# Row scales issued inside the projection, the second decay and the key packing earlier, forget gates and transposed copies on ScalarE

## The chip, the cores and the metric

The kernel runs on one core of one Trainium2 chip. The metric is device time in microseconds of one execution. A core has five engines that matter here: TensorE (PE, matmuls; its weight loads are listed as PEld), VectorE (DVE), ScalarE (ACT), GpSimd (POOL) and SyncE (SP, which issues nearly all DMAs). Each works through its own queue in order; an instruction whose operands aren't there holds up everything behind it in its queue.

## The reference

Two layers over 256 tokens of width 2048, in FP32: layer 0 mixes with HGRN2, layer 1 with gated linear attention (GLA); each also attends to 256 memory tokens, and is followed by a SwiGLU FFN.

```python
def _chunk_gated_linear_attention(q, k, v, log_a):   # S_t = diag(a_t) S_{t-1} + k_t v_t^T ; o_t = S_t^T q_t
...
def _hgrn2_mixer(hn, w_in, lb, onorm):
    proj = hn @ w_in
    q, f, i, g, xq = jnp.split(proj, [...], axis=-1)
    f = lb + (1.0 - lb) * jax.nn.sigmoid(f.astype(f32))
    log_f = jnp.log(f)
    k = 1.0 - f
    q = jax.nn.silu(q.astype(f32))
    o = _chunk_gated_linear_attention(q, k, i, log_f)            # 12 heads of 128
    y = _gated_head_norm(o, onorm, g, HGRN_HEADS)

def _gla_mixer(hn, w_in, w_gk, b_gk, onorm):
    proj = hn @ w_in
    q, k, v, g, gk_low, xq = jnp.split(proj, [...], axis=-1)
    log_a = jax.nn.log_sigmoid((gk_low @ w_gk + b_gk).astype(f32)) / 16
    o = _chunk_gated_linear_attention(q * DK ** -0.5, k, v, log_a)  # 4 heads
    y = _gated_head_norm(o, onorm, g, GLA_HEADS)
...
for layer in range(DEPTH):
    hn = _rmsnorm(h, norm_mix[layer])
    y, xq = mixer(hn)
    xa = _memory_attention(xq, mem_n, w_mem_kv[layer])           # softmax(q k^T) v over the memory
    h = h + jnp.concatenate([y, xa], axis=-1) @ w_out[layer]
    hn = _rmsnorm(h, norm_ffn[layer])
    gate, up = jnp.split(hn @ w_gate_up[layer], 2, axis=-1)
    h = h + (jax.nn.silu(gate) * up) @ w_down[layer]
return _rmsnorm(h, norm_final)
```

## The kernel before

**Products.** Every FP32 product is made from rounded parts: a weight chunk `raw` that a DMA brought is cast by ACT (`CAST parts<-raw`, the high half) and DVE subtracts (`parts<-raw,parts`, the low half); PE then does three products (high by high, high by low, low by high), the high half first. The parts lie in a ring of six buffers, the raw chunks in one of three. Some weight columns are worked in a form with fewer products (names with c and d, such as parts34c and parts34d), for which DVE adds and subtracts raw chunks first (`raw<-raw`).

**Order.** In the FFN the order of the instructions is kept as written. In the mixers a list scheduler orders each engine's queue by the program's dependences and its own estimates, so that an edit in one place can change the order elsewhere. Side work is queued with `later(...)` and issued piece by piece between the weight chunks of a projection.

**Row scales.** The RMS norm's row factor r is not applied to h but to the outputs of a projection. `h_scale` sums the squares (`rx_red`, `rm_red` on DVE), turns them with two tiny matmuls on PE (`rx_back`, `rm_back`) and makes r (`rx_v`, `rx_r`; `rm_v`, `rm_r`). rx belongs to layer 0, whose first projection is `hx`; rm to layer 1, whose first is `gx`, behind the last FFN product `fd`.

**HGRN.** Three groups of four heads. The group's gates `fs` and queries `qs` get their activations on ACT (each with an ACT_TABLE_LOAD), are turned by PE (`tf`, `tq`), and become `F` (the forget gate), `K` = 1 - F and `Q`. `decays` multiplies F into a tree (`Th`). `gated_scores` then makes the scores by levels: the even diagonal (`slh` with `k1h`), pairs (`sph`), levels 2 to 6 (`slh`), and `across` (`pxh`); `place` copies each into `sch` by mask, `grow` multiplies K and Q by the next product of decays, and `pack` copies the keys of the next level into a home, which is half of F, from the third level on. Values `vs` and `gates` come from the same projection (`hv0p` to `hv2p`; `hf1p` and `hf2p` are the next group's).

**GLA.** Two pairs of heads with the same scores (`GF`, `GK`, `GQ`, `Tg`, `slg`, `scg`). `decay(pr)` makes GF out of the matmuls `zp`: abs (`ab`) and min, Exp, Ln, a subtraction, Exp. decay(0) is issued behind the attention, decay(1) behind the scores of pair 0. The readout `gpo` gets its squares from ACT (`junk_go`), its factor (`gro_v`, `gro_r`), the gate (`ggate`), and PE turns it (`ty`).

**Attention to the memory.** Turned keys `kT`, queries `xT` and probabilities `pT` come out of PSUM by DVE copies, two of 128x512 each.

The lines named L151 in the profile are a wrapper that issues every instruction; the tile names tell them apart.

Of the kernel before, what the change touches and what calls it, by code (L numbers as in the profile page):

```python
# [17 lines left out]
P = 128  # L18
# [22 lines left out]
def trunk_kernel(ctx: ExitStack, tc: tile.TileContext, x, mem, norm_mix, norm_ffn, norm_mem,  # L41
# [694 lines left out]
    for l in range(2):  # L736
        kv = side([P, 2, XH * T], f"kv{l}")
        kT.append(kv[:, 0, :].rearrange("p (h t) -> p h t", t=T))
        vm.append(kv[:, 1, :].rearrange("p (m c) -> p m c", c=XA))
        ks = work.tile([P, NT, XA], F32, tag="stg", name=f"ks{l}", bufs=2)  # L740
        project_two(memq["pairs"], MEM[l], w_mem_kv[l], 0, XA, XA, f"m{l}",
                    lambda: [lambda t: ks[:, t, :], lambda t: vm[l][:, t, :]], prep=prep_mem if l == 0 else None)
        if l == 0:
            later(*[lambda p=p: more_of(memq, p, "hq", f"mem{p}") for p in range(len(PAIRS))
                    if f"{p}S" in MEM[1] and f"{p}S" not in MEM[0]])
            rm = mem_scale()
            load_params()
            hq, ss, first_turns = {}, new_ss("ss_x"), []
            for q in range(NQ):

                h_quad(hq, q, g_mix[0], ss, "hx", later if q > 1 else first_turns.append)
        for d in (ks, vm[l]):
            for t in range(NT):
                ac.activation(out=d[:, t, :], in_=d[:, t, :], func=AF.Copy, scale=rm[:, t:t + 1])

        def turn_keys(l=l, ks=ks):
            for j in range(2):
                tp = transposes([lambda t, c=2 * j + i: ks[:, t, c * P:(c + 1) * P] for i in range(2)], f"tk{l}{j}")
                ve.tensor_copy(kT[l][:, 2 * j:2 * j + 2, :].rearrange("p h t -> p (h t)"), tp)

        later(turn_keys)

# [4 lines left out]
    def attention(l, ps, r, yq):  # L767
# [7 lines left out]
        def turn_queries():  # L775
            st["xT"] = xT = work.tile([P, XH, T], F32, tag="Q", name=f"xT{l}")
            for j in range(2):
                tp = transposes([lambda t, c=2 * j + i: xs[:, t, c * P:(c + 1) * P] for i in range(2)], f"tx{l}{j}", True)
                ve.tensor_copy(xT[:, 2 * j:2 * j + 2, :].rearrange("p h t -> p (h t)"), tp)

        def softmax(t):
            xT = st["xT"]
# [20 lines left out]
        def turn_probs(m):  # L803
            pT = st["pT", m] = work.tile([P, XH, T], F32, tag=("T", "sc")[m], name=f"pT{l}{m}")
            for j in range(2):
                tp = transposes([lambda t, c=2 * j + i: st["prob", t][:, c, m * P:(m + 1) * P] for i in range(2)],
                                f"ap{l}{m}{j}")
                ve.tensor_copy(pT[:, 2 * j:2 * j + 2, :].rearrange("p h t -> p (h t)"), tp)

        def mix():  # L810
            quad = yq[3] = Quad("tq", f"y{l}_3")
# [13 lines left out]
    def decays(st, F, name):  # L825

        n = F.shape[2]
        st["F"] = F
        tots = work.tile([P, n * T], F32, tag="T", name=f"T{name}")
        st["T"] = {1: F.rearrange("p t n c -> p (t n c)")}  # L830
        at = 0
        for m in LEVELS[:-1]:
            tv = st["T"][m].rearrange("p (b o) -> p b o", o=2)
            nb = n * T // (2 * m)
            st["T"][2 * m] = tots[:, at:at + nb]
            ve.tensor_tensor(out=st["T"][2 * m], in0=tv[:, :, 0], in1=tv[:, :, 1], op=ALU.mult)
            at += nb

    def put_queries(st, Q, n0, ps, scale):

        n, ns = 2, Q.shape[3]
        q0, q1 = n0 * P, (ns * NT + n0) * P
        tq, tp, c = ns * P, n * P, (2, n * P // 2)
        ac.activation(out=at(Q, q0, (tq + 1, NT), c), in_=at(ps, 0, (tp + 1, NT), c), func=AF.Copy, scale=scale)
        ac.activation(out=at(Q, q1 + 2, (tq - 2, NT), (4, n * P // 4), (1, 2)),
                      in_=at(ps, 1, (tp - 1, NT), (4, n * P // 4), (2, 2)), func=AF.Copy, scale=scale)
        ve.scalar_tensor_tensor(out=at(Q, q0 + 1, (tq - 1, NT), c), in0=at(ps, 1, (tp - 1, NT), c), scalar=scale,
                                in1=at(st["T"][2], n0 * P // 2, (tq // 2, NT), (1, n * P // 2)), op0=ALU.mult, op1=ALU.mult)  # L850

    def gated_scores(st, heads, name):

# [26 lines left out]
            mult(K, 0, n * P + m, 1, n * P // m)  # L880
            mult(Q, q, n * P + m - q, 0, n * P // m + 1)

        def pack(m, home):

            n = st["K"].shape[2]
            nb = n * P // (2 * m)
            ac.copy(out=at(home, 0, (m, NT), (2 * m, nb), (1, m)), in_=at(st["K"], 0, (n * P + m, NT), (2 * m, nb), (1, m)))
            st["keys"] = home

        def score(ps, keys, q, i, parts):  # L890
            pe.matmul(ps, keys, q, start=i == 0, stop=i == len(parts) - 1)

# [8 lines left out]
        def even_diagonal():  # L901
            sc = st["sc"] = work.tile([P, ng, P], F32, tag="sc", name=f"sc{name}")
            nc.gpsimd.memset(sc, 0.0)
            pack(1, work.tile([P, st["K"].shape[2], P], F32, tag="scx", name=f"k1{name}"))
            ps = both(1, 0, 1)
            for t in range(NT):
                place(t, 0, ps[:, :, t, :], 1)
            grow(1)

        def pairs():  # L910
            for t in range(NT):
                ps = aux_ps(f"sp{name}{t}").rearrange("p (g x c) -> p g x c", x=2, c=64)
                for a, parts in enumerate(heads):
                    for i, f in enumerate(parts):
                        q = st["Q"][:, :, t, f, :].rearrange("p x (b o m) -> p x b o m", o=2, m=2)[:, :, :, 1 - t, :]
                        score(ps[:, a, :, :].rearrange("p x (b m) -> p x b m", m=2), st["K"][:, t, f, :], q, i, parts)
                place(t, 1, ps[:, 0:nh, 1, :], 1)
                place(t, 2, ps[:, 0:nh, 0, :], 2)
            grow(2)
            pack(4, st["F"][:, 1])  # L920

        def level(li):
            m = LEVELS[li]
            ps = both(m, m, -m)
            grow(m)
            if li + 1 < len(LEVELS):
                pack(2 * m, st["F"][:, li % 2])
            for t in range(NT):
                place(t, 1 + li, ps[:, :, t, :], m)

# [21 lines left out]
    def hgrn_group(w, g, hq, r, yq):  # L952
# [19 lines left out]
        def turn_f():  # L972
            F = work.tile([P, NT, 4, P], F32, tag="F", name=f"F{g}")
            K = st["K"] = work.tile([P, NT, 4, P], F32, tag="K", name=f"K{g}")
            for j in range(2):
                tp = transposes([lambda t, c=2 * j + i: fs[:, t, c * P:(c + 1) * P] for i in range(2)], f"tf{g}{j}")
                for i in range(2):
                    c = 2 * j + i
                    ve.tensor_scalar(out=F[:, :, c, :], in0=tp[:, i * T:(i + 1) * T].rearrange("p (t c) -> p t c", c=P),
                                            scalar1=oml[:, 4 * g + c:4 * g + c + 1],  # L980
                                            scalar2=lb[:, 4 * g + c:4 * g + c + 1], op0=ALU.mult, op1=ALU.add)
            ve.tensor_scalar(out=K, in0=F, scalar1=-1.0, scalar2=1.0, op0=ALU.mult, op1=ALU.add)
            decays(st, F, f"h{g}")

        def turn_q():
# [24 lines left out]
        v, gate = stages("----SSS-" if g < 2 else "----SS--", (2 * MIX, "v", AF.Copy), (3 * MIX, "gate", AF.Silu))  # L1010
        later(*([None, None, read, None, turn_y] if g < 2 else [read, None, turn_y]))

    def hgrn(hq, r, yq):
        w = hgrn_w_in[0]
        later(*first_turns)
        ps = project(hq, (2, 3, 0, 1), w, 4 * MIX, XA, "hx")
        attention(0, [[(0, ps[t])] for t in range(NT)], r, yq)
        for g in range(3):
            hgrn_group(w, g, hq, r, yq)
# [1 line left out]
    def gla_pair(w, pr, dec, decay, hq, r, yq):  # L1021
# [4 lines left out]
        def turn_k():  # L1026
            decays(st, dec[pr], f"g{pr}")
            K = st["K"] = work.tile([P, NT, 4, P], F32, tag="K", name=f"GK{pr}")
            for j in range(2):
                tp = by_tiles([lambda t, i=i: ks[:, t, j, i * P:(i + 1) * P] for i in range(2)], f"tgk{pr}{j}")  # L1030
                ac.copy(out=K[:, :, 2 * j:2 * j + 2, :].rearrange("p t h c -> p t (h c)"), in_=tp.rearrange("p (t c) -> p t c", t=NT))

        def turn_q():
            Q = st["Q"] = work.tile([P, 2, NT, 4, P], F32, tag="Q", name=f"GQ{pr}")
# [38 lines left out]
        ks, qs = dst  # L1073
        scores = gated_scores(st, [[0, 1], [2, 3]], f"g{pr}")
        if pr == 0:
            scores += [None, lambda: decay(1)]
        later(None, None, turn_k, turn_q, None, *scores)
        GLA = (("-----SS-", "-----SS-"), ("-----SS-", "-----SS-"))
        gate, v = [], []
# [10 lines left out]
                    ac.activation(out=dst[:, t, :], in_=dst[:, t, :], func=func, scale=r[:, t:t + 1])  # L1090
            later(None, None, lambda a=a: read(a), None, lambda a=a: turn_y(a))

    def gla(hq, r, yq):
        w = gla_w_in[0]
        half = (GR + XA) // 2
        kv = side([P, 2, XH * T], "kv")
# [4 lines left out]
        wgk = gk[:, 0:4, :]  # L1101
        nc.gpsimd.memset(wgk, 0.0)
        nc.sync.dma_start(out=wgk[0:GR, :, 0:DK], in_=gla_w_gk[0].rearrange("r (h c) -> r h c", c=DK))
        psx = [project(hq, range(NQ), w, 3 * MIX + i * half, half, f"gx{i}") for i in range(2)]
        low = gk[:, 4, :].rearrange("p (t c) -> p t c", c=P)
        nc.gpsimd.memset(low, 0.0)
        for t in range(NT):
# [145 lines left out]


    flush()
    r = h_scale(ss, "rx", True)
    for l in range(2):
        yq = {}
        (hgrn if l == 0 else gla)(hq, r, yq)
        hq2, ss2 = {}, new_ss(f"ss_f{l}")  # L1260
        quad_pairs(yq)
        mores = [lambda p=p, tag=tag: more_of(yq, p, tag, f"y{l}_{p}", turned[0])
# [28 lines left out]
        if l == 0:  # L1291
            hq = {}
            ffn(0, hq2, r2, lambda n: h_quad(hq, n, g_mix[1], ss, "hm1_", sevens=2))
            r = h_scale(ss, "rm1", True)
        else:
            gf = []

# [76 lines left out]
```

## Time and profile before

| | |
|---|---|
| median of 3 runs | 2276.36 us (2274.17, 2276.36, 2276.65) |
| profiled execution | 2274.12 us, span 2272.3 us, granted clock 0.999 |
| PE busy | 2250.2 us, 99% of the span |
| DVE busy | 2087.6 us, 92% |
| ACT busy | 1423.8 us, 63% |
| POOL busy | 35.3 us, 2% |
| HBM | 430.71 MB read, 191 GB/s over the span |

A row of the timeline reads: start, duration (both in us), engine, line, operation, output<-inputs, tile and shape, how many were run together, and in brackets the idle time of the engine just before it with what ended that. Layer 0's mixer lies at about 100 to 470 us of the span, layer 1's at 1215 to 1500, the FFNs behind each.

### The profile page before, as it was taken

The page shows a single profiled execution, that of the slowest core. Times are in us where ns is not written, and L with a number is a line of the kernel's source. Part 1 is how long each engine was busy: PE and PEld are TensorE (multiplying, and loading weights), DVE is VectorE, ACT ScalarE, POOL GpSimd, SP SyncE. Part 2 cuts the span into 40 slices and gives each one's busy share as a digit, 9 for nine tenths or more (in the row PEclk, how much of TensorE's full clock was granted, in tenths as well). Part 3 has the DMA queues.
Part 4 walks back from the last instruction along what each step waited for, and adds up shares of the span by engine and source line. Part 5 has one row for each costly group of instructions (what it writes and reads, how often), then busy time and mean ns, then how long its engine had stood idle before and what let it go on. Part 6 is the DMA issues. An engine that isn't in the chain of part 4 may idle for free.

```text
span 2272.3 us, 29336 instructions
## 1 busy us (share of the span) xinstructions
PE 2250.2 (99%) x10710; PEld 1900.9 (84%) x10710; DVE 2087.6 (92%) x2635; ACT 1423.8 (63%) x1940; POOL 35.3 (2%) x41
## 2 busy tenths in 40 slices
PE   9999999999999999999999999999999999999998
PEld 7888888888888888888888999988888888888887
DVE  7889999899999999999996887889899999999997
ACT  6656656566666666666665666566566666666664
POOL 0000000000000000000000000001000000000000
PEclk9999999999999999999999999999999999999999
DMA  7645545555556665556655446455555565665664
GB/s 289 204 154 179 190 161 168 179 173 186 186 195 213 207 214 191 204 192 213 207 204 161 145 140 195 152 178 204 194 196 202 205 210 196 204 206 201 205 211 158
DMA packets 232645, 435.78 MB, mean 192 GB/s; under 512 B 13200, under 2 KB 42676, under 8 KB 232244
## 3 DMA queue, kind: packets, MB, share of 16 engines
q1 hardware_dynamic: 231203, 429.64, 56.1%
q10 hardware_dynamic: 1296, 4.26, 0.5%
q8 instruction: 84, 1.38, 0.2%
q14 instruction: 62, 0.50, 0.1%
HBM read 430.71 MB, written 3.15 MB: 191 GB/s over the span
## 4 chain that ended last, share of the span: by engine, by line
PE 90%; DVE 6%; ACT 2%; issue 1%; DMA 1%; POOL 0%; SPq 0%; POOLq 0%; DVEq 0%; ACTq 0%
PE f_p L151 38%; PE fd L151 19%; PE wo L151 4%; PE m1p L151 2%; PE hf0p L151 2%; PE wo0p L151 2%; PE wo1p L151 2%; PE fd_0p L151 2%; PE gk1p L151 1%; PE gg11p L151 1%; PE gg10p L151 1%; PE m0p L151 1%; DVE raw L151 1%; PE gg00p L151 1%; PE gx L151 1%
## 5 line engine op out<-in xcount | busy, mean ns | idle before, releaser
L151 DVE TENSOR_TENSOR raw<-raw 128x512 f32<-128x512 f32 (+3 forms) x474 | 402.8, 850 | 9.4 <-DMA raw<-in_hgrn_w_in_dram 0.2
L151 DVE TENSOR_TENSOR parts<-raw,parts 128x1024 fp32r<-128x1024 f32 (+1 forms) x216 | 246.1, 1179 | 17.0 <-ACT parts L151 16.8
L151 ACT CAST parts<-raw 128x1024 fp32r<-128x1024 f32 (+1 forms) x216 | 211.6, 1016 | 46.0 <-PE gx L151 8.1
L151 ACT COPY h<-fd 128x512 f32<-128x512 f32 x80 | 46.1, 590 | 52.3 <-PE fd L151 49.5
L151 ACT ACTIVATE s<-s,rf_r 128x512 f32<-128x512 f32 x44 | 31.8, 722 | 43.7 <-DVE s L151 43.7
L151 DVE TENSOR_TENSOR e<-f_p,e 128x512 f32<-128x512 f32 x66 | 45.1, 684 | 2.3
L151 ACT COPY fd<-h 128x512 f32<-128x512 f32 x82 | 45.2, 583 | 0.0
L151 PE MATMUL fd<-parts,s_0h 128*128 128x512 f32 x128 | 39.8, 392 | 0.0
L151 PE MATMUL fd<-parts,s_6h 128*128 128x512 f32 x128 | 39.8, 392 | 0.0
L151 PE MATMUL fd<-parts,s_2h 128*128 128x512 f32 x128 | 39.8, 392 | 0.0
L151 PE MATMUL fd<-parts,s_4h 128*128 128x512 f32 x128 | 39.8, 392 | 0.0
L151 PE MATMUL fd<-parts,s_8h 128*128 128x512 f32 x128 | 39.8, 392 | 0.0
L151 PE MATMUL fd<-parts,s_5h 128*128 128x512 f32 x128 | 39.4, 389 | 0.0
L151 PE MATMUL fd<-parts,s_7h 128*128 128x512 f32 x128 | 39.4, 389 | 0.0
L151 PE MATMUL fd<-parts,s_1h 128*128 128x512 f32 x128 | 39.4, 389 | 0.0
L151 PE MATMUL fd<-parts,s_3h 128*128 128x512 f32 x128 | 39.4, 389 | 0.0
L151 DVE TENSOR_TENSOR s<-f_p,e 128x512 f32<-128x512 f32 x44 | 30.3, 688 | 4.3 <-PE f_p L151 2.4
L151 DVE SCALAR_TENSOR_TENSOR s<-e,rf_r,s 128x512 f32<-128x512 f32 x44 | 31.0, 744 | 0.2
L151 PEld LDWEIGHTS fd<-parts,s_7h 128*128 128x128 f32 x128 | 24.0, 188 | 5.0
L151 PEld LDWEIGHTS fd<-parts,s_5h 128*128 128x128 f32 x128 | 24.0, 188 | 5.0
L151 PEld LDWEIGHTS fd<-parts,s_1h 128*128 128x128 f32 x128 | 24.0, 188 | 5.0
L151 PEld LDWEIGHTS fd<-parts,s_3h 128*128 128x128 f32 x128 | 24.0, 188 | 5.0
(5722 smaller groups left out, 7229.6 us busy)
## 6 DMA issues: line engine op xcount, KB each, us to landing
raw<-in_w_gate_up_dram SPq DMA_DIRECT2D x352, 512.0 KB, 3.9
raw<-in_w_down_dram SPq DMA_DIRECT2D x80, 1024.0 KB, 5.5
raw<-in_hgrn_w_in_dram SPq DMA_DIRECT2D x96, 512.0 KB, 3.9
raw<-in_gla_w_in_dram SPq DMA_DIRECT2D x96, 384.0 KB, 3.4
raw<-in_w_out_dram SPq DMA_DIRECT2D x16, 1024.0 KB, 6.0
raw<-in_w_out_dram SPq DMA_DIRECT2D x32, 512.0 KB, 4.1
raw<-in_w_mem_kv_dram SPq DMA_DIRECT2D x30, 512.0 KB, 5.5
raw<-in_w_down_dram SPq DMA_DIRECT2D x16, 512.0 KB, 4.5
```

Of the source, the lines that this page charges most:

```text
L151: ins = func(*args, **kwargs)
```

## The change

Row scales: the two calls of `h_scale` ahead of the layers go; the mixer calls it through `prep` inside its first projection. Second decay: decay(1) goes from the end of pair 0's scores to between levels 2 and 3. Key packing: `first_keys` packs k1 where K is made; the later homes are halves of Q that are no longer read, not of F. ACT instead of DVE: F and K of HGRN, and the copies of kT, xT and pT.

```diff
-                ve.tensor_copy(kT[l][:, 2 * j:2 * j + 2, :].rearrange("p h t -> p (h t)"), tp)
+                ac.copy(out=kT[l][:, 2 * j:2 * j + 2, :].rearrange("p h t -> p (h t)"), in_=tp)
...
+    def first_keys(st, name):
+        pack(st, 1, work.tile([P, st["K"].shape[2], P], F32, tag="scx", name=f"k1{name}"))
...
-            pack(4, st["F"][:, 1])
+            pack(st, 4, st["Q"][:, 1, 1])
...
-                pack(2 * m, st["F"][:, li % 2])
+                pack(st, 2 * m, st["Q"][:, 1, li % 2])
...
-                    ve.tensor_scalar(out=F[:, :, c, :], in0=tp[:, i * T:(i + 1) * T].rearrange("p (t c) -> p t c", c=P),
-                                            scalar1=oml[:, 4 * g + c:4 * g + c + 1],
-                                            scalar2=lb[:, 4 * g + c:4 * g + c + 1], op0=ALU.mult, op1=ALU.add)
-            ve.tensor_scalar(out=K, in0=F, scalar1=-1.0, scalar2=1.0, op0=ALU.mult, op1=ALU.add)
+                    ac.activation(out=F[:, :, c, :], in_=tp[:, i * T:(i + 1) * T].rearrange("p (t c) -> p t c", c=P), func=AF.Identity,
+                                  scale=oml[:, 4 * g + c:4 * g + c + 1], bias=lb[:, 4 * g + c:4 * g + c + 1])
+            ac.activation(out=K.rearrange("p t n c -> p (t n c)"), in_=F.rearrange("p t n c -> p (t n c)"), func=AF.Identity,
+                          scale=-1.0, bias=1.0)
+            first_keys(st, f"h{g}")
             decays(st, F, f"h{g}")
...
-        ps = project(hq, (2, 3, 0, 1), w, 4 * MIX, XA, "hx")
+        got = []
+        ps = project(hq, (2, 3, 0, 1), w, 4 * MIX, XA, "hx", prep=lambda q: q == 1 and got.append(scale()))
+        r, = got
...
-            scores += [None, lambda: decay(1)]
+            scores[5:5] = [lambda: decay(1), None]
...
-        psx = [project(hq, range(NQ), w, 3 * MIX + i * half, half, f"gx{i}") for i in range(2)]
+        got = []
+        psx = [project(hq, range(NQ), w, 3 * MIX + i * half, half, f"gx{i}",
+                       prep=lambda q: len(got) == 0 and q == 3 and got.append(scale())) for i in range(2)]
+        r, = got
...
-    r = h_scale(ss, "rx", True)
+    scale = lambda ss=ss: h_scale(ss, "rx", True)
...
-            r = h_scale(ss, "rm1", True)
+            scale = lambda ss=ss: h_scale(ss, "rm1", True)
```

What this does to the queues is seen at three places. The first is PE at the seam of the layers: `fd` is the last product of layer 0's FFN, `gx` the first of layer 1. Before:

```order
L151 MATMUL fd_5_3_0_1_9664<-parts_2_9722,s_10h 128x512 x2
L151 MATMUL fd_5_3_0_1_9664<-parts_2_9722,s_10l 128x512
L151 MATMUL rm_back<-rm_red,ident 128x2
L151 MATMUL rm_back<-rm_red,turned_id 128x2
L151 MATMUL gx_0_0_9769<-parts_0_9773,hm_0x 128x264 x3
L151 MATMUL gx_0_1_9770<-parts_0_9773,hm_0x 128x264 x3
```

Now rm_back stands inside gx, behind its products with hm_5:

```order
L151 MATMUL gx_0_0_9760<-parts_2_9851,hm_5x 128x264 x3
L151 MATMUL gx_0_1_9761<-parts_2_9851,hm_5x 128x264 x3
L151 MATMUL rm_back<-rm_red,ident 128x2
L151 MATMUL rm_back<-rm_red,turned_id 128x2
L151 MATMUL gx_0_0_9760<-parts_0_9889,hm_6x 128x264 x3
```

The two matmuls moved behind the products of gx with hm_0 to hm_5.

The second place is the head of the first HGRN group on ACT. Before:

```order
L151 ACTIVATE qs_1519<-qs_1519,rx_r 128x512 x2
L151 CAST parts30b<-raw_1681 128x1024
L151 ACTIVATE Q_1612<-tq_1613 128x2x128
L151 ACTIVATE Q_1612<-tq_1613 128x2x64x2
L151 COPY k1h_1658<-K_1583 128x2x256
L151 CAST parts31a<-raw_1731 128x1024
```

Now:

```order
L151 ACTIVATE qs_1519<-qs_1519,rx_r 128x512 x2
L151 ACTIVATE F_1582<-tf_1584,lbt 128x2x128 x2
L151 ACTIVATE F_1582<-tf_1591,lbt 128x2x128 x2
L151 ACTIVATE Q_1614<-tq_1615 128x2x128
L151 ACTIVATE K_1583<-F_1582 128x1024
L151 ACTIVATE Q_1614<-tq_1615 128x2x64x2
L151 COPY k1h_1599<-K_1583 128x2x256
L151 CAST parts30b<-raw_1681 128x1024
```

F and K came in behind the activation of the queries, and the cast of parts30b moved behind them and behind k1h. In the second group the same stands on ACT, and DVE's order changes too where its values and gates are put together. Before:

```order
L151 TENSOR_TENSOR gates_2706<-hv1p_2611,vs_2705 128x512
L151 TENSOR_TENSOR parts52a<-raw_2754,parts52a 128x1024
L151 TENSOR_TENSOR vs_2705<-hv1p_2607,gates_2706 128x512
L151 TENSOR_TENSOR Q_2413<-Q_2413,Th_2400 128x2x32x8
L151 TENSOR_TENSOR gates_2706<-hv1p_2603,vs_2705 128x512
```

Now:

```order
L151 TENSOR_TENSOR vs_2705<-hv1p_2367,vs_2705 128x512
L151 TENSOR_TENSOR vs_2705<-hv1p_2371,vs_2705 128x512
L151 TENSOR_TENSOR gates_2706<-hv1p_2379,gates_2706 128x512
L151 TENSOR_TENSOR gates_2706<-hv1p_2375,gates_2706 128x512
L151 TENSOR_TENSOR parts52a<-raw_2754,parts52a 128x1024
```

The low half of parts52a, the first chunk of the third group's gates, moved from behind the first of the gates' sums to behind the last.

The third place is GLA's first pair on ACT, ahead of the first readout. Before, with decay(1) there:

```order
L151 ACT_TABLE_LOAD
L151 ACTIVATE ab_10960<-ab_10960 128x1024
L151 CAST parts245b<-raw_11128 128x2x384
L151 CAST parts245c<-raw_11128 128x2x384
L151 ACT_TABLE_LOAD
L151 ACTIVATE GF_10959<-GF_10959 128x1024
L151 ACTIVATE junk_go_11036,goss_11035<-gpo_11033 128x384
```

Now decay(1) stands among the scores of pair 0, ahead of the cast of parts238d:

```order
L151 ACTIVATE ab_10681<-ab_10681 128x1024
L151 CAST parts238b<-raw_10798 128x2x384
L151 ACT_TABLE_LOAD
L151 ACTIVATE ab_10681<-ab_10681 128x1024
L151 CAST parts238c<-raw_10798 128x2x384
L151 COPY GQ_10532<-GK_10511 128x2x8x32
L151 ACT_TABLE_LOAD
L151 ACTIVATE GF_10680<-GF_10680 128x1024
L151 CAST parts238d<-raw_10798 128x2x384
```

The Ln, the Exp and their loads moved from ahead of junk_go to ahead of the cast of parts238d; the decay's zp matmuls stand on PE where the `slg` of level 3 stood.

More of the change, by code (lines that the diff above doesn't have):

```diff
@@ L778, in turn_queries @@
                 tp = transposes([lambda t, c=2 * j + i: xs[:, t, c * P:(c + 1) * P] for i in range(2)], f"tx{l}{j}", True)
-                ve.tensor_copy(xT[:, 2 * j:2 * j + 2, :].rearrange("p h t -> p (h t)"), tp)
+                ac.copy(out=xT[:, 2 * j:2 * j + 2, :].rearrange("p h t -> p (h t)"), in_=tp)
         def softmax(t):
@@ L807, in turn_probs @@
                                 f"ap{l}{m}{j}")
-                ve.tensor_copy(pT[:, 2 * j:2 * j + 2, :].rearrange("p h t -> p (h t)"), tp)
+                ac.copy(out=pT[:, 2 * j:2 * j + 2, :].rearrange("p h t -> p (h t)"), in_=tp)
         def mix():
@@ L827, in decays @@
         n = F.shape[2]
-        st["F"] = F
         tots = work.tile([P, n * T], F32, tag="T", name=f"T{name}")
@@ L850, in put_queries, with pack @@
                                 in1=at(st["T"][2], n0 * P // 2, (tq // 2, NT), (1, n * P // 2)), op0=ALU.mult, op1=ALU.mult)
+    def pack(st, m, home):
+        n = st["K"].shape[2]
+        nb = n * P // (2 * m)
+        ac.copy(out=at(home, 0, (m, NT), (2 * m, nb), (1, m)), in_=at(st["K"], 0, (n * P + m, NT), (2 * m, nb), (1, m)))
+        st["keys"] = home
+    def first_keys(st, name):
+        pack(st, 1, work.tile([P, st["K"].shape[2], P], F32, tag="scx", name=f"k1{name}"))
     def gated_scores(st, heads, name):
@@ L881, in grow @@
             mult(Q, q, n * P + m - q, 0, n * P // m + 1)
[L883 to L888, printed above, removed]
         def score(ps, keys, q, i, parts):
@@ L903, in even_diagonal @@
             nc.gpsimd.memset(sc, 0.0)
-            pack(1, work.tile([P, st["K"].shape[2], P], F32, tag="scx", name=f"k1{name}"))
             ps = both(1, 0, 1)
@@ L1011, in hgrn_group, with hgrn @@
         later(*([None, None, read, None, turn_y] if g < 2 else [read, None, turn_y]))
-    def hgrn(hq, r, yq):
+    def hgrn(hq, scale, yq):
         w = hgrn_w_in[0]
         later(*first_turns)
-        ps = project(hq, (2, 3, 0, 1), w, 4 * MIX, XA, "hx")
+        got = []
+        ps = project(hq, (2, 3, 0, 1), w, 4 * MIX, XA, "hx", prep=lambda q: q == 1 and got.append(scale()))
+        r, = got
         attention(0, [[(0, ps[t])] for t in range(NT)], r, yq)
@@ L1031, in turn_k @@
                 ac.copy(out=K[:, :, 2 * j:2 * j + 2, :].rearrange("p t h c -> p t (h c)"), in_=tp.rearrange("p (t c) -> p t c", t=NT))
+            first_keys(st, f"g{pr}")
         def turn_q():
@@ L1091, in gla_pair, with gla @@
             later(None, None, lambda a=a: read(a), None, lambda a=a: turn_y(a))
-    def gla(hq, r, yq):
+    def gla(hq, scale, yq):
         w = gla_w_in[0]
@@ L1255, in trunk_kernel @@
     flush()
-    r = h_scale(ss, "rx", True)
+    scale = lambda ss=ss: h_scale(ss, "rx", True)
     for l in range(2):
         yq = {}
-        (hgrn if l == 0 else gla)(hq, r, yq)
+        (hgrn if l == 0 else gla)(hq, scale, yq)
         hq2, ss2 = {}, new_ss(f"ss_f{l}")
```

## Prediction

> **What bounds the kernel now.** I read the page's span and busy lines first, then the waits of TensorE (PE) in order of time, then, at each wait that the change touches, the rows of the engine that ended it.
>
> ```profile
> span 2272.3 us, 29336 instructions
> PE 2250.2 (99%) x10710; PEld 1900.9 (84%) x10710; DVE 2087.6 (92%) x2635; ACT 1423.8 (63%) x1940; POOL 35.3 (2%) x41
> ```
>
> PE is busy for 99% of the span: only some 22 us in which it stands idle can be won, and the change touches those at three kinds of place. The first is the start of layer 1.
>
> ```profile
> 1218.23 0.35 PE L151 MATMUL rm_back<-rm_red,ident 128*128 128x2 f32 x2 [2.39 <-DVE rm_red L151]
> ...
> 1217.71 0.19 ACT L151 ACTIVATION_READ_ACCUMULATOR junk_hm<-h 128x1 f32 x1
> ...
> 1217.92 0.16 DVE L151 TENSOR_REDUCE rm_red<-ss_n 128x2 f32<-128x8 f32 x1 [0.67 <-ACT junk_hm L151]
> ```
>
> The in-order PE waits 2.39 us for the row sums of h, although the projection behind it doesn't need them. The second place is the first readout of GLA.
>
> ```profile
> 1346.08 0.81 PE L151 MATMUL gpo<-gv,scg 128*128 128x384 f32 x2
> ...
> 1353.40 0.30 PE L151 MATMUL ty<-ident,ggate 128*128 128x128 f32 x1 [1.06 <-DVE gro_v L151]
> 1354.90 0.33 PE L151 MATMUL ty<-turned_id,ggate 128*128 128x128 f32 x1 [1.20 <-DVE ggate L151]
> ...
> 1348.92 1.28 ACT L151 ACT_TABLE_LOAD   x1
> 1350.21 1.06 ACT L151 ACTIVATE GF<-GF 128x1024 f32<-128x1024 f32 x1
> 1351.18 0.47 ACT L151 ACTIVATE junk_go<-gpo 128x384 bf16<-128x384 f32 x1
> ```
>
> gpo starts at 1346.08, but ScalarE (ACT) turns to its squares (junk_go) only at 1351.18, behind the second decay; ty waits 1.06 + 1.20 = 2.26 us, and with the restart of PE some 2.6. The third kind is in the three HGRN groups.
>
> ```profile
> 216.75 0.50 PE L151 MATMUL hv0p<-parts34d,hx2m 128*128 128x512 f32 x1 [0.94 <-ACT parts34d L151]
> ...
> 315.63 0.50 PE L151 MATMUL hv1p<-parts50d,hx2m 128*128 128x512 f32 x1 [0.71 <-ACT parts50d L151]
> ...
> 387.07 0.50 PE L151 MATMUL slh<-Q,k1h 128*128 128x128 f32 x2 [0.29 <-DVE Q L151]
> ...
> 410.11 0.50 PE L151 MATMUL hv2p<-parts65d,hx1m 128*128 128x512 f32 x1 [0.53 <-DVE parts65d L151]
> ```
>
> Together 2.47 us. What lies ahead of them, in the first group (busy time of PE, PEld, DVE, ACT in a stretch):
>
> ```profile
> 178.00:190.00 12.00, 12.00 (x66) 10.20 (x66) 11.20 (x21) 11.52 (x17) 0.00 (x0) 1.00 0.56 178
> 190.00:217.00 27.00, 26.06 (x126) 21.54 (x125) 26.83 (x36) 10.80 (x13) 0.00 (x0) 1.00 0.36 118
> ```
>
> At the head of a group (178 to 190) ACT is nearly full, 11.52 of 12 us; behind it VectorE (DVE) is full, 26.83 of 27. So work taken off DVE helps the late waits only if it comes back from ACT in time.
>
> **Row scales.** The two rm_back matmuls move into gx, behind its products with hm_5. PE goes from the last fd straight to gx.
>
> ```profile
> 1220.40 0.63 ACT L151 CAST parts<-raw 128x528 fp32r<-128x528 f32 x1 [2.51 <-PE gx L151]
> ...
> 1231.17 0.27 ACT L151 ACTIVATE gk<-gx,rm_r 128x16 f32<-128x16 f32 x1 [0.52 <-PE gx L151]
> ```
>
> The weights' casts wait for PE (2.51 us), not PE for them, so the supply is ahead; and rm_r is first used at 1231.17, 13 us after the sums are complete at 1217.90. Gain: 2.39 plus the restart, 2.5, of bounds 0 (later parts late by as much) and 2.5. The reduction and rm_v only change places on DVE, 0.16 each. Layer 0 had no such wait: nothing.
>
> **Second decay.** It now runs between levels 2 and 3 of pair 0. At ty the other readout shows what remains:
>
> ```profile
> 1380.07 0.62 DVE L151 SCALAR_TENSOR_TENSOR ggate<-gpo,gro_r,ggate 128x384 f32<-128x384 f32 x1 [0.72 <-POOL gro_r L189]
> ...
> 1381.39 0.27 PE L151 MATMUL ty<-ident,ggate 128*128 128x128 f32 x1
> ```
>
> With no decay ahead of it the chain ends at 1380.69 and ty starts without a wait at 1381.39, 0.7 later: the 2.6 us go. They are in part paid back where the decay lands:
>
> ```profile
> 1320.44 0.96 DVE L151 TENSOR_TENSOR parts238d<-raw,parts238d 128x768 fp32r<-128x768 f32 x1
> ...
> 1321.91 0.68 PE L151 MATMUL gg00p<-parts238d,hm_1m 128*128 128x384 f32 x3
> ...
> 1347.47 1.23 DVE L151 TENSOR_TENSOR GF<-GF,ab 128x1024 f32<-128x1024 f32 x1 [1.41 <-ACT ab L151]
> ...
> 1338.11 1.89 PE L151 MATMUL zp<-gk 128*128 128x256 f32 x8
> ...
> 1309.64 1.13 PE L151 MATMUL slg<-GQ,GF 128*128 128x128 f32 x8
> ```
>
> parts238d was ready at 1321.40 and used at 1321.91: 0.5 us of slack. Ahead of it DVE now has four more tensor_scalar of about 0.4 and GF minus ab, 1.2, with the 1.4 of idling that it had at its old place; three of the score steps, about 1.6, move behind. That is 1.6 + 1.2 + 1.4 - 1.6 = 2.6 later, so 1324.0. PE comes there later too: zp takes 1.89 where slg took 1.13, so 1322.7, and the low half is used a third of a microsecond after the high one: a new wait of 1.0. Bounds: 0, if DVE fills the idling with something else, and 2.5, if PE isn't later. Net 2.6 - 1.0 = 1.6 gained.
>
> [...]
>
> **Forget gates, F and K, and key packing.** Prices of before, mean in the middle:
>
> ```profile
> L151 DVE TENSOR_SCALAR F<-tf,lbt x12: 528/531/542, 181.2 to 382.1; 128x256 f32<-128x256 f32 x12
> L151 DVE TENSOR_SCALAR K<-F x3: 694/695/695, 183.1 to 382.6; 128x1024 f32<-128x1024 f32 x3
> ...
> L151 ACT ACTIVATE Q<-tq x12: 375/391/410, 183.7 to 386.1; 128x256 f32<-128x256 f32 x12
> ...
> L151 ACT ACTIVATE ab<-zp,pv x8: 467/475/478, 1272.7 to 1341.5; 128x256 f32<-128x256 f32 x8
> L151 ACT ACTIVATE ab<-ab x4: 1056/1062/1062, 1275.1 to 1346.4; 128x1024 f32<-128x1024 f32 x4
> ```
>
> An activation of 128x256 takes 0.39 without a per-partition operand and 0.475 with one; F has two, so I put it at 0.56 (bounds 0.39 and 0.64), 1.96 for four with some overlap; K is like ab<-ab, 1.06. DVE is rid of 1.9 + 0.6 = 2.5 us a group, ACT gets 2.9. In the first group:
>
> ```profile
> 181.52 1.34 ACT L151 ACTIVATE qs<-qs,rx_r 128x512 f32<-128x512 f32 x2
> ...
> 184.32 1.22 DVE L151 TENSOR_TENSOR parts30b<-raw,parts30b 128x1024 fp32r<-128x1024 f32 x1
> ...
> 190.07 1.32 DVE L151 COPY_PREDICATED sch<-mask,slh 128x256 f32<-128x256 uint8 x2
> 191.19 0.72 DVE L151 TENSOR_TENSOR Q<-Q,F 128x512 f32<-128x512 f32 x1
> 191.83 0.68 DVE L151 TENSOR_TENSOR parts32a<-raw,parts32a 128x512 fp32r<-128x512 f32 x1
> ```
>
> ACT is free for F at 182.8, so F ends at 184.7, K (behind one Q) at 185.95, k1h at 186.8, and the cast of parts30b, formerly ahead, at 187.75. DVE has nothing to do until F, then the Th products and K<-K,F, then waits for that cast. From 187.8: parts30b 1.14, Q 0.34, parts31a and b 2.28, the predicated copies 1.12, Q 0.64, so parts32a at 193.4 in place of 191.83: DVE is 1.6 us later although it has 2.5 less to do. From there to parts34d its list is the same, and it was full, so parts34c and d are 1.6 later too. PE now does one parts34b product first, then waits for the cast of parts34c for about 1.4 us where it waited 1.2 in all (the idle of 0.94 and the restarts): **group 0: 0.2 lost**, between 0.9 lost and 0.6 gained (F at 0.39).
>
> Group 1 is alike up to 1.7 late; the even diagonal goes nine matmuls further back, so that the Q it waits for is in time (0.2 gained), and the parts50d products too. But parts52a is now split behind the gates and values, not ahead of them:
>
> ```profile
> 319.62 1.22 DVE L151 TENSOR_TENSOR parts52a<-raw,parts52a 128x1024 fp32r<-128x1024 f32 x1
> ...
> 326.69 2.98 PE L151 MATMUL hf2p<-parts52a,hx3x 128*128 128x512 f32 x12
> ```
>
> Behind nine more operations of DVE (gates, values, a Q and two predicated copies, 5.5 us by the 0.6 that one takes of its time here), 1.6 of lateness and a pause of 1.0 for the cast of parts50d, it ends not at 320.84 but at some 328.9, and PE, which does four high products first, stands 1.8 there, against some 0.6 saved ahead: **group 1: 1.2 lost** (0.3 gained to 2.0 lost). In group 2 the wait for Q goes (0.5 with restarts), and parts65d is used later but ready later: **0.6 gained** (0 to 1.2). HGRN together: 0.8 lost. Moving the packed keys from F to Q costs no instruction; k1's copy is covered, ACT being ahead of PE there.
>
> **Copies.**
>
> ```profile
> L151 DVE COPY pT<-ap x8: 677/683/685, 146.1 to 1262.3; 128x512 f32<-128x512 f32 x8
> ...
> L151 ACT COPY h<-fd 128x512 f32<-128x512 f32 x80 | 46.1, 590 | 52.3 <-PE fd L151 49.5
> ```
>
> Sixteen copies go from 0.68 on DVE to 0.59 on ACT, and ACT is idle for 37% of the span; no wait of PE ended on them: zero; if that cover were gone, the two pT of a half, 1.2 us, would delay ao.
>
> **Sum.** 2.5 + 1.6 - 0.8 = 3.3 gained: the profiled execution took 2274.12 (2272.3 of span), which makes 2270.8. The runs before have a median of 2276.36, 2.2 above the profiled one, so against them 2273.1. What this measurement can tell from no change is about 0.2%, 4.55 us: the forecast lies within it, near its edge.
>
> **Rivals.** *The lateness of DVE is absorbed* (faster): F at the lower bound, and the reordered products hide the rest; the four HGRN waits, 2.47, go and no new one comes: 2.5 + 1.6 + 2.5 = 6.6 gained, 2269.8. For it: PE's order puts other products ahead of each late part. Against: DVE was at 99% there and starts later. *ACT bounds the HGRN groups* (slower): the late F and K are what each group then waits for. It decides from where each of the three groups loses (4.1 + 4.55) / 3 = 2.9 us, nearly twice the 1.6 to 1.7 by which DVE is late; at 3.3 each the time is 2282. For it: ACT's 11.52 of 12. Against: behind 190 ACT is 40% busy and catches up. [...] *The row scale isn't off the path* (same): gx starts early but then waits for parts or for r, 2.5 not gained: 2275.6.
>
> **Chances.** The forecast 0.48 (alone 2270.5 to 2276), absorbed 0.34, the scale without effect 0.09, ACT the bound 0.09. Faster takes the absorbed case and the forecast's lower tail, 0.40; same 0.50; slower 0.10. The range reaches from 2268, the absorbed case with group 1 at its better bound, to 2277.5, where the new waits are at their worse bounds; ACT the bound is left out.
>
> **What would show it.** No wait at rm_back, and none at ty; two table loads fewer; DVE idle for some 3 us ahead of Th in each group; waits of PE at parts34c, parts52a (the largest) and parts238d. I am wrong if parts52a and 238d come in time (faster), or if the waits of the groups exceed 2.9 us each (slower).

## The result, and the profile after

The changed kernel takes 2273.15 us (median of 12 executions, 2271.37 to 2274.62), the kernel before 2276.63 (12, 2274.17 to 2280.67): a ratio of 0.9982, 95% interval 0.9974 to 0.9989. It is faster beyond that interval, by 0.18%, and the forecast was 2273.1 (2270.8 for the profiled execution). Beside other kernels later the ratio came out as 0.998 (0.9971 to 0.9988). The profiled execution took 2273.33, 0.8 less than the one shown of before: the two traces differ by less than the medians (3.5), and why they do turned out to be the most instructive part.

The page's first lines:

```profile
span 2271.5 us, 29317 instructions
PE 2251.5 (99%) x10710; PEld 1900.6 (84%) x10710; DVE 2072.2 (91%) x2604; ACT 1437.0 (63%) x1969; POOL 36.8 (2%) x41
```

DVE lost 15 us of work, ACT gained 13 (with two table loads fewer, 13 in place of 15), and PE's time hardly moved. TensorE's timeline at the seam of the layers, and at ty:

```profile
1218.47 0.39 PE L151 MATMUL fd<-parts,s_10l 128*128 128x512 f32 x1
1218.70 1.48 PE L151 MATMUL gx<-parts,hm_0x 128*128 128x264 f32 x11
...
1351.94 2.24 PE L151 MATMUL gg01p<-parts243b,hm_5x 128*128 128x384 f32 x12
1354.02 0.27 PE L151 MATMUL ty<-ident,ggate 128*128 128x128 f32 x1
1354.13 0.27 PE L151 MATMUL ty<-turned_id,ggate 128*128 128x128 f32 x1
```

No wait is left at either place (2.39, and 1.06 + 1.20, before). Where the second decay landed, DVE and PE read:

```profile
1318.42 1.23 DVE L151 TENSOR_TENSOR GF<-GF,ab 128x1024 f32<-128x1024 f32 x1 [1.42 <-ACT ab L151]
...
1323.40 0.96 DVE L151 TENSOR_TENSOR parts238d<-raw,parts238d 128x768 fp32r<-128x768 f32 x1 [0.35 <-ACT parts238d L151]
...
1323.42 0.44 PE L151 MATMUL gg00p<-parts238d,hm_1m 128*128 128x384 f32 x1 [0.28 <-ACT parts238d L151]
1324.42 0.62 PE L151 MATMUL gg00p<-parts238d,hm_1m 128*128 128x384 f32 x2 [0.56 <-DVE parts238d L151]
```

The 1.42 of idling moved there whole, and PE waits twice; measured against its steady pace of 0.173 a matmul it loses 1.26. The switch of tables on ACT at that place:

```profile
1316.03 1.28 ACT L151 ACT_TABLE_LOAD   x1
1317.33 1.06 ACT L151 ACTIVATE ab<-ab 128x1024 f32<-128x1024 f32 x1
```

And the HGRN groups, with the form prices on ACT, DVE at the head of group 0, and PE's waits:

```profile
L151 ACT ACTIVATE F<-tf,lbt x12: 543/552/567, 182.5 to 386.4; 128x256 f32<-128x256 f32 x12
L151 ACT ACTIVATE K<-F x3: 1067/1072/1074, 184.6 to 387.1; 128x1024 f32<-128x1024 f32 x3
...
184.51 0.69 DVE L151 TENSOR_TENSOR Th<-F 128x512 f32<-128x512 f32 x1 [4.25 <-ACT F L151]
...
192.95 0.68 DVE L151 TENSOR_TENSOR parts32a<-raw,parts32a 128x512 fp32r<-128x512 f32 x1
...
216.41 0.73 PE L151 MATMUL hv0p<-parts34c,hx2m 128*128 128x512 f32 x2 [0.94 <-ACT parts34c L151]
...
330.17 2.14 PE L151 MATMUL hf2p<-parts52a,hx3x 128*128 128x512 f32 x8 [1.29 <-DVE parts52a L151]
```

DVE stands 4.25 us until F comes, and reaches parts32a at 192.95 in place of 191.83, 1.1 later although it was relieved of 2.5 us. Counted from the group's first tf, which PE starts at 180.33 in place of 180.54, it is 1.3 later. In groups 1 and 2 the wait for F is 3.15 and 3.14. The place of PE's old wait (0.94) has another of the same size, and parts52a is the new one.

### The profile page after: what moved, and what is told of

It reads as the page before. It is cut to its first block, busy times and chain, and to the rows that moved or that the text cites. A ratio compares the mean times of both kernels' runs of the same rounds, so it can differ in the third digit from the quotient of the medians.

```text
span 2271.5 us, 29317 instructions
## 1 busy us (share of the span) xinstructions
PE 2251.5 (99%) x10710; PEld 1900.6 (84%) x10710; DVE 2072.2 (91%) x2604; ACT 1437.0 (63%) x1969; POOL 36.8 (2%) x41
## 3 DMA queue, kind: packets, MB, share of 16 engines
HBM read 430.71 MB, written 3.15 MB: 191 GB/s over the span
## 4 chain that ended last, share of the span: by engine, by line
PE 86%; DVE 7%; ACT 3%; DMA 1%; issue 1%; POOL 0%; SPq 0%; DVEq 0%; POOLq 0%; ACTq 0%
PE f_p L151 39%; PE fd L151 18%; PE wo L151 4%; PE m1p L151 2%; PE wo0p L151 2%; PE wo1p L151 2%; PE m0p L151 2%; DVE raw L151 2%; PE gk1p L151 1%; PE gg11p L151 1%; PE gg10p L151 1%; PE gg01p L151 1%; PE fd_0p L151 1%; PE gx L151 1%; PE hf0p L151 1%
```

## The experiments

Twelve experiments were run; two of them are the kernels before and after, unchanged, and one kernel was run twice (u_fk, u_fk2). The stage lengths below come from one profiled execution of each: "HGRN" is from the first tx matmul to the first wo product with y_2h, "GLA" from the first slg with k1g to the first wo product of layer 1. The granted clock is the share of its full speed at which TensorE was let run; "lower" counts the executions whose mean granted clock was 0.998 or less. That is a coarse sign: the profiled execution of p_decay has a mean of 0.999, and its trace shows 0.66 over the 5 us from 1220.

| kernel | ratio to before (95%) | lower | HGRN us | GLA us |
|---|---|---|---|---|
| before, three comparisons | 1 | 74 of 97 | 323.6 | 187.3 |
| c_before | 1.0 (0.9991 to 1.0009) | 9 of 11 | 324.3 | 189.2 |
| p_scale | 0.9983 (0.9975 to 0.9992) | 7 of 11 | 324.2 | 187.8 |
| p_decay | 0.9989 (0.998 to 0.9998) | 5 of 11 | 324.7 | 186.6 |
| p_fk | 1.0005 (0.9996 to 1.0014) | 7 of 11 | 325.3 | 187.9 |
| p_copies | 1.0004 (0.9995 to 1.0013) | 10 of 11 | 323.8 | 188.8 |
| u_fk | 0.9974 (0.9965 to 0.9983) | 0 of 10 | 325.5 | 185.8 |
| u_fk2 | 0.9978 (0.9969 to 0.9988) | 0 of 9 | 324.3 | 185.8 |
| u_d8 | 0.998 (0.9971 to 0.9989) | 6 of 11 | 324.6 | 186.0 |
| scale_decay | 0.9974 (0.9965 to 0.9983) | 0 of 10 | 324.7 | 185.7 |
| d_fill | 0.9992 (0.9983 to 1.0001) | 0 of 11 | 323.7 | 186.3 |
| b_fill | 1.0011 (1.0003 to 1.002) | 1 of 12 | 325.1 | 189.2 |
| the changed kernel | 0.9982 (0.9974 to 0.9989) | 0 of 12 | 326.4 | 186.0 |
| c_after | 0.998 (0.9971 to 0.9988) | 0 of 11 | 325.5 | 185.7 |

**A second profile of before** (no edit).

> The kernel before, unchanged, as a control: what two copies of one kernel differ by here, and a second profile of it. The trace of the change shows a gain of only 0.8 us (spans 2272.3 and 2271.5), the medians show 3.5. Theory A: the first profile of before (2274.12) is a quick one of a kernel whose executions spread by some 5 us, so this profile shows the same waits in the mixers (2.39 at rm_back, 1.06 and 1.20 at ty, 0.94 at parts34d) and a span longer by 1 to 3 us with the difference in waits for DMAs, and the ratio is 1.000 within 0.001. Rival: the spread is of TensorE's pace, so every stage is longer by the same 0.1% and no wait is.

Neither theory holds as put. The wait at rm_back is the same, of the two at ty the first is longer (1.42 in place of 1.06, then 1.20 again), but what comes behind them is what differs most. Its timeline at the seam:

```profile
1219.59 0.56 PE L151 MATMUL rm_back<-rm_red,ident 128*128 128x2 f32 x2 [2.38 <-DVE rm_red L151]
1220.01 0.56 PE L151 MATMUL rm_back<-rm_red,turned_id 128*128 128x2 f32 x2
1220.44 2.99 PE L151 MATMUL gx<-parts,hm_0x 128*128 128x264 f32 x12
```

Twelve gx matmuls take 2.99 us; in the first profile of before the same twelve, behind the same wait, take 1.69. The stretches of that execution follow, in the lower part those at the waits of ty. A row gives the stretch, its length, the busy time of PE, PEld, DVE, ACT and POOL, then the granted clock, the DMA share and GB/s:

```profile
1210.00:1215.00 5.00, 5.00 (x23) 4.13 (x22) 2.50 (x6) 2.10 (x5) 0.00 (x0) 1.00 0.15 31
1215.00:1220.00 5.00, 2.62 (x12) 1.94 (x11) 2.92 (x5) 2.14 (x6) 0.00 (x0) 0.94 0.30 99
1220.00:1225.00 5.00, 5.00 (x24) 5.00 (x25) 1.03 (x3) 1.11 (x2) 0.69 (x1) 0.50 0.32 104
1225.00:1230.00 5.00, 5.00 (x38) 5.00 (x38) 3.07 (x6) 2.58 (x5) 0.00 (x0) 0.87 0.06 9
...
1355.00:1360.00 5.00, 2.38 (x13) 1.90 (x12) 3.43 (x9) 3.75 (x8) 1.35 (x2) 0.94 0.00 0
1360.00:1365.00 5.00, 5.00 (x25) 5.00 (x23) 3.94 (x8) 2.28 (x5) 0.00 (x0) 0.72 0.51 157
```

At each of the two places the granted clock falls, and comes back. From 1220 to 1225 it is 0.50 throughout, and the matmuls of tp_hm there start 0.21 us apart, in the first profile of before 0.11. If it was 0.50 at the second place too, the shares of the stretches make an estimated 6.9 and 3.4 us at half the clock, and these cost an estimated 5.2 of the 6.4 us by which this span is longer (2278.7 and 2272.3). The changed kernel keeps 1.00 in those stretches, as the first profile of before happened to do. From this came theory B, the author's guess: an idle of 2.3 to 2.4 us, such as the 2.38 at rm_back, lets the clock drop in some executions.

**The row scales alone** (the diff's edits of h_scale's calls).

> Before with the row scales' part alone. Theory A: the 2.39 us wait at rm_back goes and nothing comes in its place: span 2.5 us shorter than before's 2272.3, ratio 0.9989. Rival: later parts of gx are late instead, and the ratio is 1.000.

The wait is gone: from the last fd to the first gx it is 0.23 us in place of 3.21, and gx takes 24.61 in place of 24.25 for the two rm_back matmuls now in it, so 2.6 gained. The ratio says 3.9 us, more than the wait was long; but its interval, 1.8 to 5.7, holds the 2.6 as well.

**The second decay alone**

```diff
-            pack(4, st["F"][:, 1])
+            pack(4, st["Q"][:, 1, 1])
...
-                pack(2 * m, st["F"][:, li % 2])
+                pack(2 * m, st["Q"][:, 1, li % 2])
...
-            scores += [None, lambda: decay(1)]
+            scores[5:5] = [lambda: decay(1), None]
```

> Before with the second decay moved, and with it the packed keys' homes in Q in place of F (without which F could not be free in time). Theory A: the two waits at ty go (2.6 us), a wait of 0.8 to 1.3 us at parts238d comes: 1.3 to 1.8 us gained, ratio 0.9993. In HGRN nothing moves by more than 0.3 us. Rival: the homes in Q are what disturbs HGRN (the change lost 2.9 us there): then the HGRN stage is 1 to 3 us longer here, and the ratio 1.0005.

GLA is 0.7 shorter than in the first profile of before. HGRN is within 0.4 of c_before, though 1.1 longer than in the first profile of before, and those two differ by 0.7 themselves: that the homes disturb anything isn't shown. The wait at rm_back is still there, and in this profile too the clock fell behind it: to 0.66 over 1220 to 1225, with the matmuls of tp_hm again 0.21 us apart, which makes an estimated 3.4 us at 0.50.

**F and K on ACT alone**

```diff
-                    ve.tensor_scalar(out=F[:, :, c, :], ..., op0=ALU.mult, op1=ALU.add)
-            ve.tensor_scalar(out=K, in0=F, scalar1=-1.0, scalar2=1.0, op0=ALU.mult, op1=ALU.add)
+                    ac.activation(out=F[:, :, c, :], ..., func=AF.Identity, scale=oml[...], bias=lb[...])
+            ac.activation(out=K..., in_=F..., func=AF.Identity, scale=-1.0, bias=1.0)
```

> Before with F and K of HGRN on ScalarE alone; k1 is still packed in the scores, the homes are still in F. Theory A: F comes 1 us later, VectorE idles about 4 us ahead of Th in each group, and the mixer of layer 0 ends 2 to 3 us later; ratio 1.001. Rival: F and K cost nothing by themselves, and the 2.9 us lost there come from the earlier k1 pack and the homes: ratio 1.000.

The waits that this edit brings are there without the rest of the change:

```profile
328.23 2.12 PE L151 MATMUL hf2p<-parts52a,hx3x 128*128 128x512 f32 x8 [1.32 <-DVE parts52a L151]
```

Against its steady pace PE loses 1.48 here, as it does in the changed kernel (1.45) and in c_after (1.49), and in no kernel that keeps F and K on DVE. HGRN is 325.3; the ratio's interval holds no change as well as the loss.

**The other way round: the changed kernel with F and K on DVE**, twice.

> The changed kernel with F and K of HGRN back on VectorE, all else as changed. Theory A: HGRN's loss of 2.9 us goes, the waits at parts52a (1.29) and parts34c return to before's, and no run shows a mean clock under 0.999: 2270.2 us, ratio 0.997. Rival: most of the loss was the earlier k1 pack and the copies, which stay: 2272.5 to 2273.

> The changed kernel with F and K back on VectorE, a second time, for a comparison with the changed kernel in one call. Theory A: 1.2 to 2.4 us faster than it (HGRN's stage as in the other kernels without F and K on ScalarE). Rival: no faster than it within 0.5 us.

The parts52a wait is gone. Both are faster than before by more than the changed kernel is, by medians of 2271.85 and 2271.45 (c_after, beside the second: 2271.76), but the intervals overlap: by times alone a gain over the changed kernel isn't shown, and the rival of u_fk2 (within 0.5 us) stands by the medians. Of the traces, the three with F and K on ACT take 325.3, 325.5 and 326.4 in HGRN (c_after was expected at 325.5 to 326), the eleven without 323.6 to 325.5, median 324.3: about 1.1 us by the medians. The longest of the eleven, u_fk, lost 0.9 in front of tf, to two waits for fs (0.25 and 0.28), of which only p_decay has one.

The whole stage varies by more than that between traces, but parts of it don't. From the first hf1p matmul to the first hv1p it is 49.3 to 49.7 us in the three and 48.6 in each of the eleven; from the first hf2p, where parts52a is, to the first hv2p 50.6 in the three and 48.6 to 48.7 in the eleven. The stretches behind these give some of it back: from hv1p to hf2p the medians are 49.7 and 50.6, from hv2p to wo 74.5 and 75.0. So the loss comes from F and K, and the 1.1 is what is left of it.

**The copies alone**

```diff
-                ve.tensor_copy(xT[:, 2 * j:2 * j + 2, :].rearrange("p h t -> p (h t)"), tp)
+                ac.copy(out=xT[:, 2 * j:2 * j + 2, :].rearrange("p h t -> p (h t)"), in_=tp)
...
```

The copies of kT and pT are changed alike.

> Before with the copies of kT, xT and pT on ScalarE alone. Theory A: nothing, ratio 1.000 within 0.001, the waits at rm_back and ty as before, and the same share of runs at 0.997 to 0.998. Rival: VectorE's 4 to 5 us less work in the attention lets parts come earlier: 0.5 us faster.

No effect is seen, as expected; the ratio's interval holds the rival's 0.5 us too.

**The decay in another place** (u_fk with `scores[8:8]` in place of `scores[5:5]`).

> As u_fk, with the second decay between levels 4 and 5 in place of 2 and 3, where VectorE has no parts due at once. Theory A: the wait at parts238d (0.28 + 0.56, with restarts 1.25) goes and none comes at ty: 1.2 faster than u_fk, 2269.0. Rival: ScalarE is late for junk_go again: a wait of 1 to 2 us at ty, no faster than u_fk.

The rival was right. The wait at parts238d went, and ty has one again:

```profile
1350.57 0.27 PE L151 MATMUL ty<-ident,ggate 128*128 128x128 f32 x1
1352.14 0.33 PE L151 MATMUL ty<-turned_id,ggate 128*128 128x128 f32 x1 [1.30 <-DVE ggate L151]
```

No clock fell in its profile, yet 6 of its 11 executions were lower. Whether a wait of 1.30 is enough for that, or something else is behind it, stays open.

**The two gains alone** (row scales and second decay, nothing else of the change).

> Before with the row scales and the second decay moved (and the homes in Q), without the copies, without the earlier k1 pack and without F and K on ScalarE. Theory A: as u_fk within 0.5 us, 0.9974 of before, all runs at 0.999: these two edits are the whole gain. Rival: the copies and the earlier pack help too, and this is 0.5 to 1 us slower than u_fk.

As u_fk, with a median of 2270.56, the lowest of all: the earlier k1 pack and the copies add nothing that shows. It is the version to keep; that it beats the changed kernel (2271.76 beside it) is likely by HGRN's stage, not shown by the intervals.

**Keeping PE busy while it waits**

```diff
+            if name == "rm1":
+                for i in range(20):
+                    pe.matmul(ps[:, P:2 * P], h[:, 0, D - P:D], ident, start=True, stop=True)
             for t, by in enumerate((ident, turned_id)):
```

> Before with the second decay moved (as p_decay) and with 20 matmuls of 128x128 without use in front of rm_back, which keep TensorE busy for 2.2 us while it waits for the row sums. The wait itself stays: rm_back can't start earlier. Theory B (an idle of 2.4 us lets the clock drop to half in some executions, for 2 to 3 us of loss): all runs show a mean clock of 0.999, the median is that of p_decay's runs at 0.999, 2274.2, and the slow tail (2280) is gone. Rival: the clock drops for another reason, or the time is lost to something else: runs at 0.997 and 0.998 stay as in p_decay (5 of 11), median 2274.4 to 2275.2.

> The kernel before with 20 matmuls without use ahead of rm_back and 9 and 11 inside the two waits at ty: TensorE is busy while it waits, and the waits' ends (row sums, gate) are not moved. Theory B (the idle itself lets the clock drop in some executions): every run at a mean clock of 0.999, where before has 29 of 32 lower on one chip and 24 of 33 on the other; median 2274.5 to 2275.5, that is 0.9990 of before, with no critical work taken away. Rival: the lower clock has another cause; the share of lower runs and the median stay (2277).

The filler was twice as long as planned: the trace of d_fill has its 20 matmuls as 40, 4.73 us in place of the 2.2 that were put:

```profile
1215.29 4.73 PE L151 MATMUL rm_back<-ident,h 128*128 128x128 f32 x40
1219.85 0.28 PE L151 MATMUL rm_back<-rm_red,ident 128*128 128x2 f32 x2
```

So rm_back came 2.2 us later than it could have (from the last fd to the first gx 5.43 in place of 3.21), and in b_fill gpo to gpo grew by about 1.8 as well. The medians, 2276.04 and 2279.20, must be read less that, and miss what was expected of them. The count of lower executions says more: with PE busy none of d_fill is lower (p_decay, the same but for the filler, on another chip: 5 of 11), and one of 12 of b_fill is (before, beside it on the same chip: 21 of 32). Less its 4.0 us of filler b_fill would by estimate be at 2275.2, 1.6 under before beside it; d_fill less 2.2 at 2273.8, 0.5 under p_decay. So in these runs the lower clock goes with PE standing idle.

## Why the prediction was right, and where only its sum was

**Row scales**, 2.5 forecast: 2.6 by the stages of p_scale. No later part of gx was late.

**Second decay**, 2.6 won and 1.0 paid: both waits at ty went (from the first gpo of one readout to the first of the next it is 26.6 us in place of 29.2), and 1.26 was paid at parts238d, 0.3 more, because the cast there was late by 0.28 as well. That leaves 1.3. GLA as a whole took 185.7 to 186.6 in the seven traces with the decay there, against 187.3 to 187.9 in the three with it at the old place, no filler and no fall of the clock in that stage: 2.0 by the medians. The forecast, 1.6, lies between. The table switch took 1.30 from the start of the load to the next activation (1.29 before).

**HGRN**, 0.8 lost: about 1.1. The prices were right (F 0.552 against 0.56, K 1.07 against 1.06) and so was the mechanism, DVE idle for F and late although relieved: 1.3 late, counted from the first tf, where 1.6 was put. Group 0 was put at 0.2 lost: at parts34c PE lost 1.10 (forecast 1.4), less than before's 1.2, but 0.27 came at parts36a and 0.2 more than before at parts42d, which were not in the sum; the stretch from hf1p to hv1p is 0.7 longer by the medians. Group 1's wait at parts52a came where it was put, 1.29, or 1.45 against the steady pace, forecast 1.8; with its neighbours it makes the stretch 1.9 longer, and the one ahead is 0.8 shorter: 1.1 lost, forecast 1.2. In group 2 the wait for Q went and parts65d's stayed, 0.67 against the steady pace: from hv2p to wo 0.5 gained, forecast 0.6. Two traces alone would have said 2.9 lost, since the first profile of before had the shortest HGRN stage of the eleven, and that of the changed kernel the longest of the three.

**Copies**, zero: none is seen in p_copies.

**What the sum left out.** It priced each wait at its length and took the clock to be 1.00 throughout, as the page had it. The waits' terms as measured make 2.6 - 1.1 and 1.3 to 2.0 for the decay: 2.8 to 3.5, around the forecast's 3.3. But the means are 2277.2 for before (97 executions) and 2272.5 for the changed kernel (23), 4.6 apart; of before, the 23 executions at 0.999 have a mean of 2274.9, 2.4 from the changed kernel, and the other 2.2 come from the executions with a lower clock. That 2.4 is somewhat under the waits' terms, which the runs leave open. That before's median was 2.2 above its profiled execution was in the prediction's text, and was carried over as a fixed offset; very likely it was this, though the clocks of those first executions are not on record. The forecast kept that offset for the changed kernel too (2270.8 and 2273.1), which hid the omission: the changed kernel has no such offset, its profile being at 2273.33, 2.5 above the forecast for it, and its median at 2273.15. That the number came out to 0.1 us is in part this chance.

**The rivals.** ACT did not bound the groups: the largest new wait is 1.29, not 2.9 in each. The edit of F and K does cost, 1.1, though for F it is the place in ACT's queue and not the price (0.55 on ACT against 0.53 on DVE; K 1.07 against 0.69). The lateness of DVE was not absorbed either, and the scale was on the path.

## What to carry to other kernels

Where TensorE is busy for 99%, look for an instruction with a far supplier that stands in its queue ahead of work that needs nothing (rm_back, 2.39 us of wait), and move it behind that work. Work taken off a full engine helps only if it comes back in time: F and K left DVE 2.5 us lighter per group and in the first 1.3 later. And one profile is one execution: take a second of the same kernel, and read the granted clock behind each wait, before a difference of 1 us is given a cause.

## What the runs showed of the hardware

Behind the wait of 2.38 or 2.39 us at rm_back the granted clock fell in some executions (to 0.50 over 1220 to 1225 in c_before, to 0.66 over the same stretch in p_decay and p_copies) and not in others (1.00 there in before and p_fk). If each fall is to 0.50, the shares of the stretches make four of the five falls in the traces an estimated 3.4 us long, which at half the clock costs an estimated 1.7, and one 6.9, which costs 3.4: by that estimate the wait cost 4.1 to 5.8 us in these executions, about twice its length. The clock fell at the two shorter waits at ty too: with 1.42 and 1.20 in c_before (0.94 over 1355 to 1360, 0.72 over 1360 to 1365), and with 2.3 us of idling from 1350 to 1360 in p_copies (0.77 and 0.89); and p_scale, which has only these, has 7 lower executions of 11. A thousandth of mean clock went with about 2.3 us (2274.46, 2277.17 and 2279.03 at 0.999, 0.998 and 0.997 in the first comparison), about a thousandth of the time. The kernels without any of these waits kept 0.999 or more in 52 executions of 52. Why the clock falls in some executions of a kernel and not in others, and what sets how long it stays down, the runs do not show.
